# PEER block, dense part: one of the four one-hot products per build step moved from VectorE to ScalarE, key lists searched in another order, activations and gates loaded earlier

## The chip, the cores and the metric

One core of one Trainium2 chip runs the whole program. The time is the device time of one execution in microseconds, the median over several runs; a lower time is better. The engines that matter here are TensorE (PE in the profile), VectorE (DVE), ScalarE (ACT), GpSimd (POOL, which issues the gathers) and SyncE (SP, which issues most loads).

## The reference, cut to what matters

Two transformer blocks run on 512 tokens of 1024 features. The second ends with PEER, a layer of 16384 small experts that are addressed by two lists of 128 keys in each of 8 heads. This is the part that the change touches:

```python
def peer(xn, wq, subkeys, u_tab, v_tab):
    q = (xn @ wq).reshape(bsz, s, PEER_HEADS, 2, PEER_HALF)
    sub = jnp.einsum('bshpd,hpnd->bshpn', q, subkeys, preferred_element_type=jnp.float32)
    s_top, i_top = lax.top_k(sub, PEER_TOPK)
    cand = (s_top[..., 0, :, None] + s_top[..., 1, None, :]).reshape(bsz, s, PEER_HEADS, PEER_TOPK * PEER_TOPK)
    cand_idx = (i_top[..., 0, :, None] * N_KEYS + i_top[..., 1, None, :]).reshape(...)
    best, pos = lax.top_k(cand, PEER_TOPK)
    expert = jnp.take_along_axis(cand_idx, pos, axis=-1)
    gate = jax.nn.softmax(best, axis=-1)
    ...
        a = jax.nn.gelu(jnp.einsum('td,ted->te', xb, u_tab[eb]))
        return jnp.einsum('te,ted->td', (gb * a).astype(vb.dtype), v_tab[eb])
```

There are 16 lists of 128 scores for each block of 128 tokens (8 heads, two halves), so 64 lists in all, and 16 of each are kept.

## The kernel before, in words

The 512 tokens are four blocks of 128, called tb 0 to 3. For the tokens of tb 0, tb 1 and the first half of tb 2 (320 tokens) every expert is computed densely; the other 192 tokens gather their experts' rows from memory.

**Precise matmuls.** `unit()` loads a 128x1024 block of weights on SP's queue, casts the high half on ScalarE (L138, `whi`) and subtracts the low half on VectorE (L140, `wlo`), in rings of four; `mm3` makes each product as three matmuls (L156 to L158). So each block of weights passes ScalarE, then VectorE, then TensorE.

**Query stage.** Sixteen projections give the queries; after each, TensorE makes the key scores `sub`. Between them `advance(route, ...)` hands out pieces of the generator `routed()`, whose first pieces search the lists of tb 2 and 3 (`top_keys`, five VectorE instructions for a list).

**u stage.** A loop over 50 pairs of expert blocks calls `u_block` 100 times: 24 matmuls of 128x320, then a gelu on ScalarE into `ab` (L879). Four such blocks are stored to `a_dram` at a time. Beside each block the loop advances `routed()` by the time `R_US` and the gathers by `GATHER`. `routed()` makes, in this order: `keys` of tb 2 and of tb 3, the 32 lists of tb 0 and 1, `keys` and `build` of tb 0, the same of tb 1, `weights2` (which needs all 64 of the first gathers, L891), and `build` of tb 2.

**Build steps.** A step of `build` serves 8 tokens. VectorE makes two one-hot tiles (`oh1` L1036, `oh2` L1037) and two products of `oh2`, with the high half of the gates (`ohh`) and with the low half (`ohl`), both in L1043. TensorE multiplies them into two banks, 8 tokens by two 128x128 f16 matmuls (L1050); ScalarE moves each bank to `gt` (L1051). There are 40 such plain steps (16 for tb 0, 16 for tb 1, 8 for tb 2); eight "made" steps of tb 2 have three products. Every second step ends with two copies to `gres` (L1055) and a store to `g_dram`.

**v stage.** For each of 128 expert blocks `v_block` runs 18 matmuls of 128x512. `first` fetches stored activations (`al`) from `a_dram` or computes the block there and then; `second` fetches a group of gates (`gl`, one for eight blocks) and multiplies the two on VectorE (L1170), then splits the product (L152, L153). These loads stand in SP's queue among those of the weights. The later gathers (L899, L906) run beside it.

Each engine carries out its instructions in one fixed list, which the framework's scheduler writes when the program is built; the numbers that `yield` hands to `advance` set how many pieces of `routed()` stand beside each block.

Of the kernel before, what the change touches and what calls it, by code (L numbers as in the profile page):

```python
# [9 lines left out]
F32 = mybir.dt.float32  # L10
# [13 lines left out]

TOP_US = 5.0

R_US = 3.6
GATHER = 0.5
G_US = 2.3
NSPILL = 100  # L30
# [30 lines left out]
def tile_layers(ctx: ExitStack, tc: tile.TileContext, A: dict, out: bass.AP):  # L61
# [161 lines left out]
    def zipped(*gs):  # L223
        gs = list(gs)
        while gs:
            for g_ in list(gs):
                t = next(g_, None)
                if t is None:
                    gs.remove(g_)
                else:  # L230
                    yield t
# [621 lines left out]
    drp = pool("peerd", space=DRAM)  # L853
    h_dram = drp.tile([3, 128, 1024], F32, name="h_dram")
    g_dram = drp.tile([16 - N_RES, 128, 24, 8, 16], F32, name="g_dram")
    a_dram = drp.tile([32, 128, 4, N_U], F32, name="a_dram")

    def xs4(tb):
        if tb < 3:
# [61 lines left out]
    def keys(pr, tb):  # L921
# [83 lines left out]
        for j in range(2):  # L1005
            T.transpose(pt[:, 256 + j * 128:384 + j * 128], sl[:, j], ident)
        S.copy(sTs[tb], pt.rearrange("p (a t) -> p a t", a=4))
        if tb == 2:
            S.activation(gT2, pt[:, 320:384], AF.Copy, scale=2.0 ** -14)
        yield 3.0  # L1010
# [13 lines left out]
    def build(pr, tb):  # L1024

        sT = sTs[tb]
        for ts in range(8):
            gt = pr.tile([128, 128, 16], F32, name="gt", bufs=2)
            for t8 in range(0, 16, 8):
                made = tb == 2 and ts >= 4  # L1030
                part = lambda x, t: x[:, t:t + 8].rearrange("p (g q) -> p g q", g=4)[:, :, None, :].to_broadcast([128, 4, 128, 2])
                t0 = ts * 16 + t8
                oh1 = pr.tile([128, 4, 128, 2], F16, name="oh1", bufs=2)
                oh2 = pr.tile([128, 4, 128, 2], F16, name="oh2", bufs=1)
                io = iota16[:, None].to_broadcast([128, 4, 128, 2])
                V.tensor_tensor(oh1, io, part(sT[:, 0], t0), op=OP.is_equal)  # L1036
                V.tensor_tensor(oh2, io, part(sT[:, 1], t0), op=OP.is_equal)  # L1037
                ohs = []
                for name in ("ohh", "ohl", "ohm")[:3 if made else 2]:
                    o_ = pr.tile([128, 4, 128, 2], F16, name=name, bufs=1 if name == "ohm" else 2)  # L1040
                    o_ = o_.bitcast(BF16) if made else o_[:]
                    x_ = part(w2s[:, len(ohs)], t0 - 64) if made else part(sT[:, 2 + len(ohs)], t0)
                    V.tensor_tensor(o_, oh2, x_, op=OP.mult)  # L1043
                    ohs.append(o_)
                for q in range(2):
                    gp = bank("b").rearrange("p (t i) -> p t i", t=4)
                    for j in range(4):
                        g2, t2 = 2 * q + j // 2, j % 2
                        for o_ in ohs:
                            T.matmul(gp[:, j, :], o_[:, g2, :, t2], oh1[:, g2, :, t2], start=o_ is ohs[0], stop=o_ is ohs[-1])  # L1050
                    S.activation(gt[:, :, t8 + 4 * q:t8 + 4 * q + 4], gp.rearrange("p t i -> p i t"), AF.Copy,  # L1051
                                 scale=1.0 if made else 2.0 ** -14)
                yield 3.4 if made else 2.7
            for g in range(N_RES):
                S.copy(gres[g][:, tb * 8 + ts], gt[:, 8 * g:8 * g + 8, :])  # L1055
            nc.scalar.dma_start(g_dram[:, :, tb * 8 + ts].rearrange("g p i t -> p g (i t)"),
                                gt[:, 8 * N_RES:, :].rearrange("p (g i) t -> p g (i t)", i=8))
# [3 lines left out]
    with ExitStack() as st:  # L1061
        ptop = pool("ptop", stack=st)
        sTs = {tb: ptop.tile([128, 4, 128], F16, name=f"sT{tb}") for tb in (0, 2)}
        sTs[1] = sTs[0]
        gT2 = ptop.tile([128, 64], F32, name="gT2")
        w2s = ptop.tile([128, 3, 64], BF16, name="w2s")
        zg = ptop.tile([128, 128], F32, name="zg")
# [16 lines left out]
               pk.tile([128, 16, 128], F32, name=f"sub{tb}") for tb in range(4)]  # L1084
        skT = pk.tile([128, 16, 128], F32, name="skT")
        nc.scalar.dma_start(skT, A["skT"])
        todo = []

        def routed():
            while todo or not keyed:  # L1090
                if todo:
                    yield from todo.pop(0)
                else:
                    yield 0.0
            st2.close()
            pr = pool("pr", stack=st)
            yield from keys(pr, 2)
            yield from keys(pr, 3)
            for tb in (0, 1):
                yield from top_keys(sub[tb], tb, range(16))  # L1100
            for tb in (0, 1):
                yield from keys(pr, tb)
                yield from build(pr, tb)
            while not made2:
                next(gat)
            weights2()
            yield 0.5
            yield from build(pr, 2)
# [4 lines left out]
        for c4 in range(4):  # L1113
            sb_ = [bank("b") for _ in range(4)]
            for j in range(4):
                hp = c4 * 4 + j
                qc = pk.tile([128, 512], F32, name="qc", bufs=2)
                S.copy(qc, pr4[j] if c4 == 0 else proj_T(next_unit(), xhi, xlo))
                for tb in range(4):
                    T.matmul(sb_[tb][:, j * 128:(j + 1) * 128], qc[:, tb * 128:(tb + 1) * 128], skT[:, hp, :],  # L1120
                             start=True, stop=True)
                if c4:
                    d1 = advance(route, d1 + TOP_US)
            for tb in range(4):
                S.copy(sub[tb][:, c4 * 4:c4 * 4 + 4, :], sb_[tb].rearrange("p (a n) -> p a n", a=4))
            todo += [top_keys(sub[tb], tb, range(c4 * 4, c4 * 4 + 4)) for tb in (2, 3)]
        keyed.append(True)
        for n4 in range(0, 2 * len(SPAIR), 4):
            ab = ptop.tile([128, 4, N_U], F32, name="ab", bufs=2)
            for j in range(4):  # L1130
                u_block(2 * SPAIR[(n4 + j) // 2] + j % 2, ab[:, j, :], "a")

                if ready:
                    g1 = GATHER * (2 - len(made2))
                    d2 = advance(gat, d2 + g1)
                d1 = advance(route, d1 + R_US - (g1 if ready else 0.0))
            nc.scalar.dma_start(a_dram[n4 // 4], ab)
        for _ in route:
            pass

    with ExitStack() as st:
        pv = pool("pv", stack=st)
        yb_ = [[bank("a") for _ in range(2)] for _ in range(2)] + [[bank("b") for _ in range(2)]]
        state = {"debt": 0.0}

        def first(p, j):

            if j == 0:
                if p in SPAIR:
                    n = SPAIR.index(p)  # L1150
                    if n % 2 == 0:
                        state["al"] = pv.tile([128, 4, N_U], F32, name="al", bufs=2)
                        nc.sync.dma_start(state["al"], a_dram[n // 2])
                    state[p] = state["al"][:, 2 * (n % 2):2 * (n % 2) + 2, :]
                else:
                    state[p] = pv.tile([128, 2, N_U], F32, name="av", bufs=2)
            if p not in SPAIR:
                u_block(2 * p + j, state[p][:, j, :], "b")

        def second(p):  # L1160

            i1 = 2 * p
            if i1 % 8 == 0 and i1 // 8 < N_RES:
                state["gl"] = gres[i1 // 8]
            elif i1 % 8 == 0:
                state["gl"] = pv.tile([128, 24, 8, 16], F32, name="gl", bufs=2)
                nc.sync.dma_start(state["gl"], g_dram[i1 // 8 - N_RES])
            av = state.pop(p)
            g4 = state["gl"][:, :, i1 % 8:i1 % 8 + 2, :]
            V.tensor_tensor(g4[:, 0:N_U // 16], av.rearrange("p b (s t) -> p s b t", t=16), g4[:, 0:N_U // 16], op=OP.mult)  # L1170
            whi = pv.tile([128, 2, 384], F32R, name="wvhi", bufs=3)
            wlo = pv.tile([128, 2, 384], F32R, name="wvlo", bufs=3)
            split(whi.rearrange("p b (s t) -> p s b t", t=16), wlo.rearrange("p b (s t) -> p s b t", t=16), g4)
            return whi, wlo

        def v_block(i1, w):
            vu = unit(A["peer_v"][i1 * 128:(i1 + 1) * 128, :])
            for tb in range(3):
                for hf in range(2):
                    mm3(yb_[tb][hf], w[0][:, i1 % 2, tb * 128:(tb + 1) * 128], w[1][:, i1 % 2, tb * 128:(tb + 1) * 128],  # L1180
                        vu[0][:, hf * 512:(hf + 1) * 512], vu[1][:, hf * 512:(hf + 1) * 512], i1 == 0, i1 == 127)

        for j in range(2):
            first(0, j)
        w = second(0)
        first(1, 0)
        for p in range(64):
            g_us = G_US if p in SPAIR else 1.5 * G_US
            if p < 63:
                first(p + 1, 1)  # L1190
                wn = second(p + 1)
            v_block(2 * p, w)
            state["debt"] = advance(gat, state["debt"] + g_us)
            if p < 62:
                first(p + 2, 0)
            v_block(2 * p + 1, w)
            state["debt"] = advance(gat, state["debt"] + g_us)
            w = wn
# [138 lines left out]
```

## Time and profile before

| what | us |
|---|---|
| median of 3 runs (lowest, highest) | 2135.93 (2133.8, 2136.33) |
| the profiled execution, own time | 2130.1 |
| its span in the trace | 2128.4 |
| TensorE busy (share) | 2048.3 (96%) |
| VectorE busy (share) | 1575.3 (74%) |
| ScalarE busy (share) | 821.0 (39%) |
| GpSimd busy (share) | 524.3 (25%) |

The span is that of the trace; the execution's own time is 1.7 us longer. Busy time is a sum over instructions, and matmuls overlap, so a stage is better read by its stretches. Stretches that the text names, in us from the start of the span: the query stage 946 to 1047, the u stage 1051 to 1480 (its part with `keys` and lists until 1229, its part with build steps from there), the v stage 1500 to 2121.

### The profile page before, as it was taken

Reading aid. Unit: us, or ns where it says so; the run is one execution under the profiler, and the core shown is the slowest. Engines: PE = TensorE matmul, PEld = TensorE weight load, DVE = VectorE, ACT = ScalarE, POOL = GpSimd, SP = SyncE. Lnnn points to the kernel's source line nnn. Section 1 sums busy time; section 2 is a strip of 40 time slices with the busy share of each in tenths; the row PEclk is TensorE's granted clock in tenths of the full one; section 3 lists DMA queues with packets and bytes.
Section 4 is the critical chain, followed back from the end, with each engine's and each line's share of the span. In section 5 each row is a group of like instructions: output and inputs, shape, how many; then the busy total and the mean of one; then the engine's idle time right before and its main releaser. Section 6 shows DMA issues by size and latency. Waiting matters only on the chain.

```text
span 2128.4 us, 29432 instructions
## 1 busy us (share of the span) xinstructions
PE 2048.3 (96%) x11104; PEld 1743.5 (82%) x11104; DVE 1575.3 (74%) x2880; ACT 821.0 (39%) x1303; POOL 524.3 (25%) x383
## 2 busy tenths in 40 slices
PE   7979999999988999999989999999999999999999
PEld 6737888888876877888889899999888878788887
DVE  6994633332259955455699999998898988899997
ACT  4364422221244342333453455555333333233332
POOL 1000100000010000000032222220575666566573
PEclk9989999999999999999999999999999999999999
DMA  5202233333222222333278899899999999999996
GB/s 190 78 21 89 80 99 98 92 98 118 81 79 80 75 84 70 109 124 99 84 282 280 288 301 359 295 364 303 373 393 410 392 404 392 410 391 410 412 405 241
DMA packets 163282, 476.47 MB, mean 224 GB/s; under 512 B 13866, under 2 KB 57266, under 8 KB 161219
## 3 DMA queue, kind: packets, MB, share of 16 engines
q1 hardware_dynamic: 67104, 259.70, 34.4%
q0 software_dynamic: 46656, 169.18, 20.8%
q10 hardware_dynamic: 49378, 45.71, 6.3%
q8 instruction: 87, 1.43, 0.3%
q14 instruction: 57, 0.46, 0.1%
HBM read 432.18 MB, written 42.09 MB: 223 GB/s over the span
## 4 chain that ended last, share of the span: by engine, by line
PE 25%; DVE 18%; issue 14%; DMA 10%; POOL 3%; ACT 1%; DVEq 0%; POOLq 0%; SPq 0%; ACTq 0%
PE bank_a L158 5%; PE bank_a L156 5%; PE bank_a L157 5%; DVE wlo L140 5%; DMA rows<-in_peer_u_dram,gidx 3%; POOL rows L883 3%; DMA rows<-in_peer_v_dram,gidx 3%; DVE rows L899 2%; DMA al<-a_dram 2%; PE bank_b L156 2%; PE bank_b L157 2%; PE bank_b L158 2%; DVE rows L891 2%; PE bank_b L1050 1%; DMA raw<-in_ut_dram 1%
## 5 line engine op out<-in xcount | busy, mean ns | idle before, releaser
L138 ACT CAST whi<-raw 128x1024 fp32r<-128x1024 f32 (+1 forms) x413 | 431.9, 1047 | 891.4 <-PE bank_a L157 327.3
L140 DVE TENSOR_TENSOR wlo<-raw,whi 128x1024 fp32r<-128x1024 f32 (+1 forms) x413 | 500.1, 1214 | 274.1 <-ACT whi L138 271.8
L156 PE MATMUL bank_a<-xhi,whi 128*128 128x320 f32 (+2 forms) x1600 | 548.2, 344 | 1.0 <-ACT xhi L152 0.8
L158 PE MATMUL bank_a<-xhi,wlo 128*128 128x320 f32 (+2 forms) x1600 | 545.1, 341 | 4.0 <-DVE wlo L140 3.7
L157 PE MATMUL bank_a<-xlo,whi 128*128 128x320 f32 (+2 forms) x1600 | 547.1, 342 | 0.6 <-DVE xlo L153 0.6
L883 POOL DMA_INDIRECT rows<-in_peer_u_dram,gidx x192 | 280.9, 1463 | 554.2 <-DVE gidx L984 145.0
L158 PEld LDWEIGHTS bank_a<-xhi,wlo 128*128 128x128 f32 x1600 | 302.2, 189 | 32.9 <-DVE wlo L140 6.0
L156 PEld LDWEIGHTS bank_a<-xhi,whi 128*128 128x128 f32 x1600 | 301.6, 189 | 29.3 <-issue 2.0
L157 PEld LDWEIGHTS bank_a<-xlo,whi 128*128 128x128 f32 x1600 | 302.7, 189 | 27.1 <-DVE xlo L153 1.6
L883 POOL DMA_INDIRECT rows<-in_peer_v_dram,gidx x128 | 207.0, 1617 | 115.2 <-DVE h L906 90.3
L164 POOL TENSOR_TENSOR rstd<-rstd,neghalf 128x1 f32<-128x1 f32 (+2 forms) x37 | 26.6, 720 | 826.2 <-DVE rstd L163 818.2
L156 PE MATMUL bank_a<-whi,wvhi 128*128 128x512 f32 x512 | 201.1, 393 | 8.2 <-ACT wvhi L152 8.1
L158 PE MATMUL bank_a<-whi,wvlo 128*128 128x512 f32 x512 | 201.4, 393 | 1.9 <-DVE wvlo L153 1.9
L157 PE MATMUL bank_a<-wlo,wvhi 128*128 128x512 f32 x512 | 200.6, 392 | 2.4 <-DVE wlo L140 2.4
L906 DVE SCALAR_TENSOR_TENSOR h<-rows,ga,h 128x1024 f32<-128x1024 f32 x128 | 164.3, 1284 | 5.2 <-DMA rows<-in_peer_v_dram,gidx 4.2
L899 DVE SCALAR_TENSOR_TENSOR rows<-rows,h 128x1024 f32<-128x1024 f32 x128 | 152.8, 1220 | 7.7 <-DMA rows<-in_peer_u_dram,gidx 7.7
L156 PEld LDWEIGHTS bank_a<-whi,wvhi 128*128 128x128 f32 x512 | 96.9, 189 | 29.1 <-ACT wvhi L152 10.2
L158 PEld LDWEIGHTS bank_a<-whi,wvlo 128*128 128x128 f32 x512 | 96.7, 189 | 25.1 <-DVE wvlo L153 5.1
L157 PEld LDWEIGHTS bank_a<-wlo,wvhi 128*128 128x128 f32 x512 | 96.8, 189 | 22.4 <-DVE wlo L140 3.2
L157 PE MATMUL bank_b<-wlo,wvhi 128*128 128x512 f32 x256 | 99.6, 389 | 0.0
L156 PE MATMUL bank_b<-whi,wvhi 128*128 128x512 f32 x256 | 99.6, 389 | 0.0
L158 PE MATMUL bank_b<-whi,wvlo 128*128 128x512 f32 x256 | 99.6, 389 | 0.0
(400 smaller groups left out, 3255.2 us busy)
## 6 DMA issues: line engine op xcount, KB each, us to landing
raw<-in_wt_dram SPq DMA_DIRECT2D x150, 512.0 KB
raw<-in_ut_dram SPq DMA_DIRECT2D x128, 512.0 KB
raw<-in_peer_v_dram SPq DMA_DIRECT2D x128, 512.0 KB
g_dram<-gt ACTq DMA_DIRECT2D x24, 896.0 KB
gl<-g_dram SPq DMA_DIRECT2D x14, 1536.0 KB
a_dram<-ab ACTq DMA_DIRECT2D x25, 640.0 KB
al<-a_dram SPq DMA_DIRECT2D x25, 640.0 KB
rows<-in_peer_u_dram,gidx POOLq DMA_INDIRECT x192
```

The lines of the kernel that those rows point to most:

```text
L138: lead[0] = S.copy(hi[:, :n], raw[:, :n]).ins
L140: pace[0] = V.tensor_tensor(lo[:, :n], raw[:, :n], hi[:, :n].bitcast(F32), op=OP.subtract).ins
L156: T.matmul(o, lh, rh, start=start, stop=False)
L157: T.matmul(o, lh, rl, start=False, stop=False)
L158: T.matmul(o, ll, rh, start=False, stop=stop)
L164: G.tensor_tensor(r, r, neghalf[:, :shape[1]], op=OP.pow)
L883: G.indirect_dma_start(out=r, out_offset=None, in_=table, in_offset=bass.IndirectOffsetOnAxis(ap=idx[:, k:k + 1], axis=0))
L891: V.scalar_tensor_tensor(r, r, 1.0, hn2, op0=OP.mult, op1=OP.mult, accum_out=ga2[:, k:k + 1])
L899: V.scalar_tensor_tensor(r, r, 1.0, hn3, op0=OP.mult, op1=OP.mult, accum_out=ga[:, k:k + 1])
L906: V.scalar_tensor_tensor(h[3], r, ga[:, k:k + 1], h[3], op0=OP.mult, op1=OP.add)
L1050: T.matmul(gp[:, j, :], o_[:, g2, :, t2], oh1[:, g2, :, t2], start=o_ is ohs[0], stop=o_ is ohs[-1])
```

## The change

It does four things. (1) In the 40 plain build steps the product with the low half of the gates, one VectorE instruction of 128x1024, becomes eight ScalarE instructions of 128x128, each scaled by one column of `glo`, a new f32 copy of the low halves; `oh2` gets a second buffer. (2) The lists are kept in two queues, in pieces of two; those of tb 0 and 1 can now be searched in the query stage when those of tb 2 and 3 have been, and what is left of them alternates with `keys` of tb 2 and 3. (3) `R_US` becomes 3.3, and a plain step's `yield` 2.1. (4) Activations are stored and loaded in pairs, loaded four pairs ahead into five buffers; a group of gates is loaded three pairs earlier.

```diff
-R_US = 3.6
+R_US = 3.3
@@
         S.copy(sTs[tb], pt.rearrange("p (a t) -> p a t", a=4))
+        S.copy(glo[tb], pt[:, 384:512])
@@
-                oh2 = pr.tile([128, 4, 128, 2], F16, name="oh2", bufs=1)
+                oh2 = pr.tile([128, 4, 128, 2], F16, name="oh2", bufs=2)
@@
-                    V.tensor_tensor(o_, oh2, x_, op=OP.mult)
+                    if made or name == "ohh":
+                        V.tensor_tensor(o_, oh2, x_, op=OP.mult)
+                    else:
+                        for t in range(8):
+                            S.mul(o_[:, t // 2, :, t % 2], oh2[:, t // 2, :, t % 2], glo[tb][:, t0 + t:t0 + t + 1])
@@
-                yield 3.4 if made else 2.7
+                yield 3.4 if made else 2.1
@@
-            yield from keys(pr, 2)
-            yield from keys(pr, 3)
-            for tb in (0, 1):
-                yield from top_keys(sub[tb], tb, range(16))
+            yield from zipped(chain(keys(pr, 2), keys(pr, 3)), chain(*todo[1]))
@@
-            todo += [top_keys(sub[tb], tb, range(c4 * 4, c4 * 4 + 4)) for tb in (2, 3)]
+            for tb in (2, 3, 0, 1):
+                todo[tb < 2] += [top_keys(sub[tb], tb, range(c4 * 4 + j, c4 * 4 + j + 2)) for j in (0, 2)]
@@
-        for n4 in range(0, 2 * len(SPAIR), 4):
-            ab = ptop.tile([128, 4, N_U], F32, name="ab", bufs=2)
+        for n, p in enumerate(SPAIR):
+            ab = ptop.tile([128, 2, N_U], F32, name="ab", bufs=2)
@@
-            nc.scalar.dma_start(a_dram[n4 // 4], ab)
+            nc.scalar.dma_start(a_dram[n], ab)
@@
+        def load_a(p):
+
+            if p in SPAIR:
+                state[p] = pv.tile([128, 2, N_U], F32, name="al", bufs=5)
+                nc.sync.dma_start(state[p], a_dram[SPAIR.index(p)])
+
+        def load_g(g):
+
+            if g < N_RES:
+                state["g", g] = gres[g]
+            elif g < 16:
+                state["g", g] = pv.tile([128, 24, 8, 16], F32, name="gl", bufs=2)
+                nc.sync.dma_start(state["g", g], g_dram[g - N_RES])
@@
-            if i1 % 8 == 0 and i1 // 8 < N_RES:
-                state["gl"] = gres[i1 // 8]
-            elif i1 % 8 == 0:
-                state["gl"] = pv.tile([128, 24, 8, 16], F32, name="gl", bufs=2)
-                nc.sync.dma_start(state["gl"], g_dram[i1 // 8 - N_RES])
+            if i1 % 8 == 0:
+                state["gl"] = state.pop(("g", i1 // 8))
+            if i1 % 8 == 2:
+                load_g(i1 // 8 + 1)
@@
+            if 5 <= p + 4 < 64:
+                load_a(p + 4)
             v_block(2 * p, w)
```

The first place is ScalarE's list in the build steps of tb 0. Before, it holds these rows (`ab` is the gelu after a block of 24 matmuls, `whi` the cast that a later block needs, `gt` the copies that a build step's matmuls end with):

```order
L879 ACTIVATE ab<-bank_a 128x320
L138 CAST whi<-raw 128x1024 x2
L879 ACTIVATE ab<-bank_a 128x320
L1051 ACTIVATE gt<-bank_b 128x128x4 x2
L1137 DMA a_dram<-ab 128x1280
L138 CAST whi<-raw 128x1024
L879 ACTIVATE ab<-bank_a 128x320
L1051 ACTIVATE gt<-bank_b 128x128x4 x2
L1055 COPY gres_6485<-gt 128x128
L1055 COPY gres_6486<-gt 128x128
L1056 DMA g_dram<-gt 128x14x128
```

The casts stand two to four blocks ahead of the gelus there: the tile that is cast between two gelus is not that of the next block. After the change, the pattern that repeats for two blocks and two steps is this one:

```order
L879 ACTIVATE ab<-bank_a 128x320
L1048 ACTIVATE ohl<-oh_10365,glo_7070 128x128 x3
L1056 ACTIVATE gt<-bank_b 128x128x4 x2
L1143 DMA a_dram<-ab 128x640
L138 CAST whi<-raw 128x1024
L1048 ACTIVATE ohl<-oh_10437,glo_7070 128x128 x8
L1056 ACTIVATE gt<-bank_b 128x128x4
L138 CAST whi<-raw 128x1024
```

There are 16 scaling instructions (L1048) in it, and the number of casts ahead has shrunk: from the fifth block of a build on, the first of these two casts is that of the very next block, and it stands behind the gelu of the block before and behind both copies of the step between them.

The second place is VectorE's list ahead of `weights2`, where the last of the first gathers (L891) are taken in. Before:

```order
L1043 TENSOR_TENSOR ohl<-oh_12326,sT_7068 128x1024
L891 SCALAR_TENSOR_TENSOR rows,ga_6475<-rows,h_71 128x1024
L140 TENSOR_TENSOR wlo<-raw,whi 128x1024
L891 SCALAR_TENSOR_TENSOR rows,ga_6475<-rows,h_71 128x1024 x4
L899 SCALAR_TENSOR_TENSOR rows,ga<-rows,h_70 128x1024
```

And after:

```order
L1038 TENSOR_TENSOR oh_12463<-iota_7088,sT_7069 128x1024
L140 TENSOR_TENSOR wlo<-raw,whi 128x1024
L891 SCALAR_TENSOR_TENSOR rows,ga_6475<-rows,h_71 128x1024 x15
L140 TENSOR_TENSOR wlo<-raw,whi 128x1024
L891 SCALAR_TENSOR_TENSOR rows,ga_6475<-rows,h_71 128x1024 x2
L1037 TENSOR_TENSOR oh_12462<-iota_7088,sT_7069 128x1024
```

Fifteen gather products now stand between two low halves of weights, where four and one stood.

Counted over the same lists: of the 32 lists of tb 0 and 1 none stood in the query stage before, and 14 do now. `build` of tb 0 began after 44 gelus of the u stage and begins after 37 now; before, build steps stood beside the blocks up to the end of the stage, and now the last seven blocks have none beside them.

The third place is SP's queue at the start of the v stage, as a difference:

```order
-L1153 DMA al<-a_dram 128x1280
+L1156 DMA al<-a_dram 128x640 x2
 L134 DMA raw<-in_peer_v_dram 128x1024
-L1153 DMA al<-a_dram 128x1280
-L1167 DMA gl<-g_dram 128x3072
+L1156 DMA al<-a_dram 128x640 x2
+L1164 DMA gl<-g_dram 128x3072
 L134 DMA raw<-in_ut_dram 128x1024
 L134 DMA raw<-in_peer_v_dram 128x1024
-L1167 DMA gl<-g_dram 128x3072
+L1156 DMA al<-a_dram 128x640 x2
+L1164 DMA gl<-g_dram 128x3072
```

The same bytes are loaded, in pieces of half the size, and a piece stands further ahead of the block that uses it.

## Rows read from the trace of the kernel before

**Rows 1.** Stretches by stage: start, length, busy us of each engine (instructions), clock, DMA

```profile
946.00:1047.00 101.00, 100.76 (x567) 85.80 (x566) 49.09 (x212) 33.04 (x49) 0.00 (x0) 1.00 0.29 92
1051.00:1229.00 178.00, 166.77 (x1171) 161.21 (x1171) 174.38 (x675) 81.30 (x113) 44.61 (x36) 0.99 0.76 269
1229.00:1480.00 251.00, 247.30 (x2154) 241.29 (x2153) 247.34 (x435) 142.42 (x261) 50.92 (x41) 0.99 0.95 326
1500.00:2121.00 621.00, 608.01 (x2854) 512.78 (x2853) 563.26 (x639) 209.72 (x236) 386.77 (x240) 0.99 0.99 390
```

**Rows 2.** Waits of TensorE, 1051 to 1480: us in total, times, longest

```profile
PE bank_b L976 <- DVE ohl L973: 9.3, 5, 2.5
PE bank_a L158 <- DVE wlo L140: 3.7, 7, 0.9
```

**Rows 3.** Waits of TensorE and of VectorE, 1500 to 2121

```profile
PE bank_a L156 <- ACT wvhi L152: 8.1, 3, 3.6
...
DVE gl L1170 <- DMA al<-a_dram: 20.1, 5, 4.8
...
DVE gl L1170 <- DMA gl<-g_dram: 5.6, 3, 3.1
```

**Rows 4.** Timeline of ScalarE in the build part: start, us, instruction

```profile
1261.06 1.05 ACT L138 CAST whi<-raw 128x1024 fp32r<-128x1024 f32 x1 [1.86 <-PE bank_a L157]
1262.01 0.43 ACT L879 ACTIVATE ab<-bank_a 128x320 f32<-128x320 f32 x1
1262.34 0.59 ACT L1051 ACTIVATE gt<-bank_b 128x512 f32<-128x512 f32 x1
...
1262.82 0.60 ACT L1051 ACTIVATE gt<-bank_b 128x512 f32<-128x512 f32 x1
1263.45 0.30 ACT L1055 COPY gres<-gt 128x128 f32<-128x128 f32 x1
...
1263.65 0.29 ACT L1055 COPY gres<-gt 128x128 f32<-128x128 f32 x1
```

**Rows 5.** ScalarE's scaling by a column elsewhere in the program: timeline, and group

```profile
19.61 0.98 ACT L344 ACTIVATE dg<-cst,cw 128x128 f32<-128x128 f32 x3
...
L344 ACT ACTIVATE dg<-cst,cw 128x128 f32<-128x128 f32 x8 | 3.0, 397 | 1.5 <-PE bank_b L345 1.4
```

**Rows 6.** Timeline of TensorE in the build part (ten f16 matmuls between the first two rows)

```profile
1232.55 0.22 PE L1050 MATMUL bank_b<-oh,ohh 128*128 128x128 f16 x1
...
1233.18 0.22 PE L1050 MATMUL bank_b<-oh,ohh 128*128 128x128 f16 x1
...
1233.49 0.30 PE L157 MATMUL bank_a<-xlo,whi 128*128 128x320 f32 x1
1233.64 0.31 PE L158 MATMUL bank_a<-xhi,wlo 128*128 128x320 f32 x1
```

**Rows 7.** Timeline of VectorE ahead of `weights2`

```profile
1404.51 1.22 DVE L140 TENSOR_TENSOR wlo<-raw,whi 128x1024 fp32r<-128x1024 f32 x1
1405.64 1.22 DVE L891 SCALAR_TENSOR_TENSOR rows<-rows,h 128x1024 f32<-128x1024 f32 x1
...
1406.79 1.22 DVE L891 SCALAR_TENSOR_TENSOR rows<-rows,h 128x1024 f32<-128x1024 f32 x1
...
1411.37 0.68 DVE L1036 TENSOR_TENSOR oh<-iota,sT 128x1024 f16<-128x1024 f16 x1
1411.98 0.68 DVE L1037 TENSOR_TENSOR oh<-iota,sT 128x1024 f16<-128x1024 f16 x1
```

**Rows 8.** Groups of VectorE by shape, 1051 to 1480: busy us, mean ns

```profile
L915 DVE FIND_INDEX8 si<-sv,gres 128x8 uint32<-128x128 f32 x32 | 9.2, 287 | 0.0
L914 DVE MAX8 sv<-gres 128x8 f32<-128x128 f32 x32 | 8.9, 282 | 0.0
```

**Rows 9.** TensorE after a wait: timeline (in brackets the idle time before), and the stretch behind it

```profile
1325.93 0.61 PE L976 MATMUL bank_b<-ident,ohl 128*128 128x128 f16 x4 [2.50 <-DVE ohl L973]
...
1326.00:1329.40 3.40, 3.40 (x22) 3.25 (x23) 2.65 (x6) 1.91 (x2) 0.00 (x0) 0.51 0.69 278
```

More of the change, by code (lines that the diff above doesn't have):

```diff
@@ L855, in tile_layers @@
     g_dram = drp.tile([16 - N_RES, 128, 24, 8, 16], F32, name="g_dram")
-    a_dram = drp.tile([32, 128, 4, N_U], F32, name="a_dram")
+    a_dram = drp.tile([64, 128, 2, N_U], F32, name="a_dram")
     def xs4(tb):
@@ L1064, in tile_layers @@
         sTs[1] = sTs[0]
+        glo = {tb: ptop.tile([128, 128], F32, name=f"glo{tb}") for tb in (0, 2)}
+        glo[1] = glo[0]
         gT2 = ptop.tile([128, 64], F32, name="gT2")
@@ L1086, in tile_layers @@
         nc.scalar.dma_start(skT, A["skT"])
-        todo = []
+        todo = [[], []]
         def routed():
-            while todo or not keyed:
-                if todo:
-                    yield from todo.pop(0)
+            while todo[0] or not keyed:
+                if todo[0] or todo[1]:
+                    yield from (todo[0] or todo[1]).pop(0)
                 else:
@@ L1125, in tile_layers @@
                 S.copy(sub[tb][:, c4 * 4:c4 * 4 + 4, :], sb_[tb].rearrange("p (a n) -> p a n", a=4))
-            todo += [top_keys(sub[tb], tb, range(c4 * 4, c4 * 4 + 4)) for tb in (2, 3)]
+            for tb in (2, 3, 0, 1):
+                todo[tb < 2] += [top_keys(sub[tb], tb, range(c4 * 4 + j, c4 * 4 + j + 2)) for j in (0, 2)]
         keyed.append(True)
-        for n4 in range(0, 2 * len(SPAIR), 4):
-            ab = ptop.tile([128, 4, N_U], F32, name="ab", bufs=2)
-            for j in range(4):
-                u_block(2 * SPAIR[(n4 + j) // 2] + j % 2, ab[:, j, :], "a")
+        for n, p in enumerate(SPAIR):
+            ab = ptop.tile([128, 2, N_U], F32, name="ab", bufs=2)
+            for j in range(2):
+                u_block(2 * p + j, ab[:, j, :], "a")
                 if ready:
@@ L1144, in tile_layers @@
         state = {"debt": 0.0}
-        def first(p, j):
[L1148 to L1156, printed above, removed]
+        def load_a(p):
[8 more added lines that the diff above has]
+                nc.sync.dma_start(state["g", g], g_dram[g - N_RES])
+        def first(p, j):
+            if j == 0 and p not in SPAIR:
+                state[p] = pv.tile([128, 2, N_U], F32, name="av", bufs=2)
             if p not in SPAIR:
@@ L1181, in v_block @@
                         vu[0][:, hf * 512:(hf + 1) * 512], vu[1][:, hf * 512:(hf + 1) * 512], i1 == 0, i1 == 127)
+        load_g(0)
+        for p in range(5):
+            load_a(p)
         for j in range(2):
```

## The prediction

> **What bounds the kernel now.** I read the stretches by stage first. In the query stage TensorE is busy for 100.8 of 101 us and VectorE for only 49 [rows 1]: TensorE sets the time and VectorE has half the stage free. In the part of the u stage with keys and lists VectorE is busy for 174.4 of 178 us and TensorE for 166.8, so VectorE sets the time there; the waits say the same, 9.3 us of TensorE behind the one-hot products of `keys` and 3.7 us behind low halves of weights [rows 2]. In the build part both are full, TensorE 247.3 and VectorE 247.3 of 251, while ScalarE is busy for 142.4 [rows 1]. TensorE's own work there is close to that: a matmul of 128x320 starts 0.147 us after the one before (1233.49, 1233.64 and on), so a block of 24 takes 3.53 us; eleven f16 matmuls from 1232.55 to 1233.18 make 0.057 each, so a plain step of 16 takes 0.92 and a made one of 24 takes 1.38 [rows 6]. In the v stage TensorE is busy for 608 of 621 us [rows 1], and what it waits for most is the high half of the gated activations, 8.1 us in three waits; VectorE waits 20.1 us for `al` and 5.6 us for `gl` ahead of the product from which that half is made [rows 3].
>
> So there is little to win: 178 − 167 and 251 − 247 in the u stage, some 15 us, and 13 us in the v stage.
>
> **Lists in the query stage.** A list is five instructions of about 0.28 us each (8.9 and 9.2 us for 32) [rows 8], 1.4 us busy, 1.2 with their overlap. Fourteen of them go into the query stage: 17 to 20 us beside 49 busy of 101, hidden by TensorE's projections. I cost that at 0; if they delayed low halves there, at most the 20 us that they take.
>
> **Keys and lists in the u stage.** This part is now beside 37 blocks instead of 44. VectorE loses the 14 lists (17) and seven blocks' low halves and gathers, 7 x (1.13 + 1.15) = 16 [rows 7]: 174.4 − 33 = 141. TensorE needs 37 x 3.53 = 131 plus the matmuls of `keys` (166.8 − 44 x 3.53 = 11.5): 142. I take 142 us.
>
> **ScalarE in the build steps.** One VectorE product costs 0.61 us (1411.37 to 1411.98) [rows 7]; 40 of them are 24 us, taken from an engine that is full. In their place stand 320 scalings of 128x128 by a column. Three of that kind elsewhere take 0.98 us with 0.397 for one, so they start (0.98 − 0.40)/2 = 0.29 apart [rows 5]. The lower bound is a copy of the same size without the column, 0.20 apart (1263.45, 1263.65) [rows 4]; the upper one is the whole 0.40. I take 0.29, the row of the same operation. For two blocks and two steps ScalarE then has two casts (0.95 apart), two gelus (0.33), four `gt` copies (0.48), two `gres` copies (0.20) [rows 4] and 16 scalings: 2 x 1.28 + 1.92 + 0.40 + 4.64 = 9.5 us (8.1 at 0.20, 11.3 at 0.40). TensorE needs 2 x (3.53 + 0.92) = 8.9. The sum alone is nearly a tie.
>
> The Trainium skill, "ScalarE: Activation LUTs", Rules for kernel authors, says to put a plain product on VectorE, and budgets about 0.3 us for an instruction with a pointer operand plus 0.83 ns per element. By it one scaling would be an estimated 0.41 us, which is the 0.397 that the row gives for one by itself but not the 0.29 between starts; the sum for two blocks would be 11.4 us instead of 9.5.
>
> What costs more than the sum is the order. ScalarE's list shows the cast of the next block behind the gelu of the block before, which needs the end of that block on TensorE, and behind both `gt` copies. So the chain closes on itself once for two blocks: the last matmul's tail 0.16 (0.31 long, next start 0.15 later) [rows 6], gelu 0.33, three scalings 0.87, two `gt` 0.96, cast 1.05 [rows 4], low half 1.22 [rows 7], then the block's other 22 matmuls 3.23 with half a step 0.46 between, and the next block 3.53: **11.8 us** in place of 8.9, 2.9 lost each time. At a scaling of 0.20 it is 11.5, and without the wait for the low half (two matmuls run ahead of it) not under 10.8, a loss of 2. Before, the casts stood two to four blocks ahead, so the chain was open.
>
> **The u stage summed.** Keys 142. Each of the two long builds spans 16 blocks; the first four have their casts ahead (17.8 at 8.9 a pair), and the other twelve are six closed pairs, 71: 89 each, 178. `keys` of tb 1 between them, 8 blocks, 30. Then `weights2`: 17 gather products in two runs stand ahead of the low halves, 17 x 1.15 = 19.5 [rows 7], of which a block in hand covers 3.5, so 16 lost; the plain steps of tb 2 beside six blocks, 27 at TensorE's pace plus about one closed pair 3: 46. Eight made steps with ten blocks, 10 x 3.53 + 8 x 1.38 = 46. Seven blocks with nothing beside them, 25. Together 467 us against 178 + 251 = 429: **+38**. The last seven blocks are where VectorE's saved time ends up: the routing is finished early, and nothing is there to shorten.
>
> The second `oh2` costs no time by itself: VectorE's one-hots would otherwise wait for ScalarE's readers. The copy into `glo` (three, at most 0.6 each) lies in VectorE's time. A smaller `R_US` with a smaller yield only sets the order that is counted above.
>
> **The v stage.** Activations four pairs ahead and gates three take away VectorE's 20.1 + 5.6 [rows 3]; what reaches the end is bounded by TensorE's idle time, 621 − 608 = 13, and starts at 0 since DMA is busy for 0.99 of the stage [rows 1]: a load that is issued earlier then takes its share from the weights. I take **−9**, the 8.1 behind the high half and some of the rest [rows 3]. Loads of half the size are not slower by anything that a row shows.
>
> **The sum.** 38 − 9 = +29. The profiled execution had 2130.1 of its own, so 2159; the median of the runs shown is 5.8 higher, so **2165**.
>
> **Rivals.**
> (a) *The casts keep their lead on the chip.* If fewer pairs are closed than I count, the change gains. Without any, the u stage is 467 − 13 x 2.9 = 429, no change, and with −9 the time is 2127, faster. It turns at about three closed pairs (3 x 2.9 = 9). For it: VectorE loses 24 + 17 us of work in a stage that it fills. Against: a list is carried out in order, and 13 such pairs stand in it. The Trainium skill, "Perfetto Trace Analysis", Optimizing Scalar/DVE Operations, says that moving work to ScalarE may make sense where VectorE is saturated. By that rule it would be this case; the trace agrees on the 98%, and it shows TensorE equally full.
> (b) *The closed pairs cost less, since gather products and pieces of `keys` are drawn into the gaps.* At 2 us for 13 pairs (−12), 8 for the run of gathers (−8), and all 13 us of the v stage (−4) the time is 2141, just slower; with ScalarE at 0.20 as well, within the bound of no change, 2136.
> (c) *TensorE's clock drops in the gaps.* After a wait of 2.50 us it ran at 0.51 of its full clock for 3.4 us, losing 1.7 [rows 9]. The gap in a closed pair is about 2.1 (second `gt` 0.48, cast 1.05, and the way to them), followed by two matmuls and a wait for the scalings. If it drops in each, 14 x 1.7 = 24: 2189.
> (d) *The earlier loads bring nothing*, because the queues are as full as before: +9, 2174.
>
> **How the numbers follow.** A chance of 0.52 for the forecast (its own range 2152 to 2178), 0.11 for (a), 0.11 for (b), 0.15 for (c), 0.11 for (d). The range from 2137 to 2189 leaves out (a) and the upper end of (c). Time differences under 0.2% (4 us) can't be told from no change by a measurement of this kernel. Faster: (a) and a small part of (b), 0.13. Same: half of (b), 0.06. Slower: 0.81.
>
> **What will show it.** In the u stage after: the scalings 0.29 us apart; the waits of TensorE led by high halves from ScalarE's cast (L138), 2 us at a time in the builds, some 12 of them, where before there were none; pairs of gelus 11.8 apart instead of 9; one idle stretch of TensorE of some 16 us ahead of `weights2`; the first to the last gelu 467 us. The keys part would be 142 long and the last seven blocks 3.5 each. In the v stage the waits for `al` and `gl` are gone and TensorE is idle for 4 us instead of 13. The prediction is wrong if the gelus in the builds keep a distance of 4.5 us (then (a)), or if the granted clock shows halves all along the builds (then (c)).

## The result and the profile after

The changed kernel takes 2223.28 us (median of 4 runs, 2219.39 to 2224.01) against 2134.86 for the kernel before in the same series: ratio 1.0415, 95% interval 1.04 to 1.0429. It is slower, as forecast, but by 88 us where 29 were summed; the time lies above the range.

The stretches of the changed kernel by stage: start and end, length, busy us of PE, PEld, DVE, ACT, POOL (instructions), clock, DMA share, GB/s. They answer to [rows 1].

```profile
946.00:1047.00 101.00, 100.76 (x567) 85.83 (x567) 66.26 (x324) 32.77 (x48) 0.00 (x0) 1.00 0.29 93
1051.00:1193.00 142.00, 131.86 (x958) 130.31 (x958) 140.14 (x573) 70.18 (x98) 28.47 (x24) 0.98 0.74 257
1193.00:1585.00 392.00, 335.56 (x2416) 302.55 (x2416) 254.70 (x397) 249.20 (x605) 72.78 (x57) 0.89 0.76 249
1605.00:2215.00 610.00, 603.28 (x2827) 509.91 (x2827) 552.82 (x623) 208.84 (x234) 370.88 (x233) 0.99 0.98 388
```

The query stage took 17 us more of VectorE's work at no cost. All of the loss is in the build part: TensorE busy for 336 of 392 us, where it was busy for 247 of 251, and its granted clock 0.89. The first and the last gelu of the u stage, before and then in the changed kernel:

```profile
L879 ACT ACTIVATE ab<-bank_a x100: 421/433/479, 1050.9 to 1479.6; 128x320 f32<-128x320 f32 x100
```

```profile
L879 ACT ACTIVATE ab<-bank_a x100: 410/436/443, 1051.2 to 1584.6; 128x320 f32<-128x320 f32 x100
```

So the u stage, from the first to the last of them, is 533.4 us long instead of 428.7: +104.7. What lies behind it is 637.6 instead of 648.8: −11.2. TensorE's waits in the u stage of the changed kernel (total, times, longest):

```profile
PE bank_b L1055 <- DVE ohh L1045: 24.6, 15, 1.7
PE bank_a L158 <- DVE wlo L140: 9.5, 4, 8.9
PE bank_b L1055 <- ACT ohl L1048: 8.8, 17, 1.7
PE bank_a L156 <- ACT whi L138: 8.6, 4, 2.7
...
PE bank_b L1006 <- DVE slot L1001: 6.3, 1, 6.3
```

The first row names a VectorE product, fifteen times up to 1.7 us. It is the release that came last by a little; the cast that came just ahead of it is seen in the timeline of one pair of blocks, here of all engines in the changed kernel:

```profile
1262.97 0.44 ACT L879 ACTIVATE ab<-bank_a 128x320 f32<-128x320 f32 x1 [1.66 <-PE bank_a L158]
...
1266.96 0.44 ACT L879 ACTIVATE ab<-bank_a 128x320 f32<-128x320 f32 x1 [2.10 <-PE bank_a L158]
...
1267.29 1.01 ACT L1048 ACTIVATE ohl<-oh,glo 128x128 f16<-128x128 f16 x3
...
1268.34 0.69 DVE L1038 TENSOR_TENSOR oh<-iota,sT 128x1024 f16<-128x1024 f16 x1 [3.66 <-ACT ohl L1048]
...
1268.64 0.59 ACT L1056 ACTIVATE gt<-bank_b 128x512 f32<-128x512 f32 x1
...
1269.12 1.05 ACT L138 CAST whi<-raw 128x1024 fp32r<-128x1024 f32 x1
...
1269.55 0.69 DVE L1045 TENSOR_TENSOR ohh<-oh,sT 128x1024 f16<-128x1024 f16 x1
...
1270.20 1.23 DVE L140 TENSOR_TENSOR wlo<-raw,whi 128x1024 fp32r<-128x1024 f32 x1
1270.29 0.29 PE L1055 MATMUL bank_b<-oh,ohh 128*128 128x128 f16 x2 [1.70 <-DVE ohh L1045]
1270.39 0.39 PE L156 MATMUL bank_a<-xhi,whi 128*128 128x320 f32 x1
...
1271.48 0.62 PE L158 MATMUL bank_a<-xhi,wlo 128*128 128x320 f32 x1
...
1271.90 0.47 PE L156 MATMUL bank_a<-xhi,whi 128*128 128x320 f32 x1
1272.17 0.47 PE L157 MATMUL bank_a<-xlo,whi 128*128 128x320 f32 x1
```

The closed pair is there, step for step: gelu, three scalings, the copies, the cast (until 1270.17), and TensorE's next matmul 0.1 us behind it. A second strand comes in at the same time: VectorE's one-hot `oh2` (L1038) waits 3.66 us until ScalarE's scalings have read the tile's older buffers, and `ohh`, the product that the next build matmul needs, is done at 1270.24, 0.07 us behind the cast. TensorE is idle for 1.70 us, and from 1271.48 its matmuls start 0.27 apart instead of the 0.147 of [rows 6]. The stretches of two such pairs, by the same columns as above:

```profile
1249.40:1263.00 13.60, 11.69 (x84) 10.40 (x82) 7.44 (x10) 9.82 (x27) 0.94 (x1) 0.87 0.71 224
1263.00:1276.60 13.60, 11.69 (x84) 10.40 (x81) 8.59 (x12) 9.79 (x27) 2.19 (x2) 0.87 0.82 237
```

A pair takes 13.6 us at a mean clock of 0.87. It holds one stretch of 3.4 us at half the clock, which costs 1.7 us at most; without it the pair is 11.9, and 11.8 was worked out. ScalarE is busy for 9.8 us in it. The scalings start 0.29 apart, as taken.

Ahead of `weights2` stand these idle times of TensorE (timeline):

```profile
1454.57 0.42 PE L156 MATMUL bank_a<-xhi,whi 128*128 128x320 f32 x1 [2.62 <-ACT whi L138]
...
1469.50 0.64 PE L158 MATMUL bank_a<-xhi,wlo 128*128 128x320 f32 x1 [8.86 <-DVE wlo L140]
```

The stretch around them:

```profile
1453.00:1478.00 25.00, 11.58 (x59) 9.65 (x60) 21.67 (x39) 8.94 (x20) 20.13 (x17) 0.59 1.00 377
```

Of 25 us TensorE works in 11.6, at a mean clock of 0.59.

### The profile page after: what moved, and what is told of

Its sections match the earlier page's. It is cut to its first block, busy times and chain, and to the rows that moved or that the text cites. A ratio compares the mean times of both kernels' runs of the same rounds, so it can differ in the third digit from the quotient of the medians.

```text
span 2222.2 us, 29782 instructions
## 1 busy us (share of the span) xinstructions
PE 2097.1 (94%) x11104; PEld 1771.2 (80%) x11104; DVE 1559.0 (70%) x2840; ACT 913.1 (41%) x1626; POOL 518.5 (23%) x383
## 4 chain that ended last, share of the span: by engine, by line
PE 34%; issue 16%; DVE 13%; DMA 4%; POOL 4%; ACT 1%; DVEq 0%; POOLq 0%; ACTq 0%; SPq 0%
PE bank_a L158 8%; PE bank_a L156 8%; PE bank_a L157 7%; POOL rows L883 4%; DVE wlo L140 3%; PE bank_b L156 3%; PE bank_b L157 3%; PE bank_b L158 3%; DVE rows L899 2%; DMA raw<-in_peer_v_dram 2%; DMA rows<-in_peer_u_dram,gidx 1%; PE bank_b L1055 1%; DVE h L906 1%; DMA raw<-in_ut_dram 1%; DVE wvlo L153 1%
## 5 line engine op out<-in xcount | busy, mean ns | idle before, releaser
L156 PE MATMUL bank_a<-xhi,whi 128*128 128x320 f32 (+2 forms) x1600 | 561.0, 352 | 9.5 <-ACT whi L138 8.6
L158 PE MATMUL bank_a<-xhi,wlo 128*128 128x320 f32 (+2 forms) x1600 | 556.6, 348 | 9.8 <-DVE wlo L140 9.5
L157 PE MATMUL bank_a<-xlo,whi 128*128 128x320 f32 (+2 forms) x1600 | 557.7, 349 | 0.6 <-DVE xlo L153 0.6
L156 PEld LDWEIGHTS bank_a<-xhi,whi 128*128 128x128 f32 x1600 | 311.5, 195 | 38.5 <-ACT whi L138 10.3
L158 PEld LDWEIGHTS bank_a<-xhi,wlo 128*128 128x128 f32 x1600 | 311.4, 195 | 37.7 <-DVE wlo L140 11.5
L157 PEld LDWEIGHTS bank_a<-xlo,whi 128*128 128x128 f32 x1600 | 312.2, 195 | 27.0 <-DVE xlo L153 1.7
L883 POOL DMA_INDIRECT rows<-in_peer_v_dram,gidx x128 | 196.9, 1538 | 119.9 <-DVE h L906 101.8
L1048 ACT ACTIVATE ohl<-oh,glo 128x128 f16<-128x128 f16 x320 | 104.6, 433 | 5.6 <-DVE oh L1038 5.5
```

The lines of the kernel that those rows point to most:

```text
L156: T.matmul(o, lh, rh, start=start, stop=False)
L157: T.matmul(o, lh, rl, start=False, stop=False)
L158: T.matmul(o, ll, rh, start=False, stop=stop)
L883: G.indirect_dma_start(out=r, out_offset=None, in_=table, in_offset=bass.IndirectOffsetOnAxis(ap=idx[:, k:k + 1], axis=0))
L1048: S.mul(o_[:, t // 2, :, t % 2], oh2[:, t // 2, :, t % 2], glo[tb][:, t0 + t:t0 + t + 1])
```

## The experiments

**The low product back on VectorE.** The changed kernel with

```diff
-                    if made or name == "ohh":
-                        V.tensor_tensor(o_, oh2, x_, op=OP.mult)
-                    else:
-                        for t in range(8):
-                            S.mul(...)
+                    V.tensor_tensor(o_, oh2, x_, op=OP.mult)
```

> The changed kernel with the low product back as one VectorE instruction (all else of the change kept, the run of 15 gather products too). Theory (the scalings let ScalarE's casts fall back to a lead of none, which closes the chain cast, block, gelu, cast, and the gaps halve TensorE's clock): pairs of gelus back at 9 us, about two half-clock periods in the u stage, u stage 425 to 440 instead of 533, median about 2125. Rival (the run of gathers ahead of weights2 and the uneven filling of the blocks cost most of it): u stage over 470, median over 2160.

2139.48 us, ratio 1.0026 (1.0015 to 1.0038). The u stage is 445.9 us, with pairs of 9.0 and one interval of 31.7 ahead of `weights2`:

```profile
L879 ACT ACTIVATE ab<-bank_a x100: 420/432/450, 1051.9 to 1497.8; 128x320 f32<-128x320 f32 x100
```

So the scalings cost 533 − 446 = 87 us, nearly the whole loss. The median is 14 above what was expected: the run of gathers keeps its price when the scalings are gone.

**The scalings without the lists.** The kernel before with the loads, the f32 copy `glo` and

```diff
-                oh2 = pr.tile([128, 4, 128, 2], F16, name="oh2", bufs=1)
+                oh2 = pr.tile([128, 4, 128, 2], F16, name="oh2", bufs=2)
@@
-                    V.tensor_tensor(o_, oh2, x_, op=OP.mult)
+                    if made or name == "ohh":
+                        V.tensor_tensor(o_, oh2, x_, op=OP.mult)
+                    else:
+                        for t in range(8):
+                            S.mul(...)
```

> The kernel before with the scalings on ScalarE and the loads of the v stage changed (which make room for the second one-hot tile), but with the lists, R_US and the yields of before; only four gather products in a row ahead of weights2. Theory: the list shows the casts without a lead here as well, so the u stage is 490 to 520 and the median about 2190 to 2210. Rival (the gather run and the filling cost most): u stage under 460, median under 2150.

2222.87 us, ratio 1.0422 (1.0404 to 1.0439), u stage 522.3: the loss comes with the scalings alone, and is 13 us above the range expected, which no run explains. No run of 15 gather products is in it. The loads by themselves take 2134.2 us (below).

**Casts two blocks ahead.** The changed kernel with

```diff
+        blocks = [2 * p + j for p in SPAIR for j in range(2)]
+        early = [unit(A["ut"][i]) for i in blocks[:2]]
@@
-                u_block(2 * p + j, ab[:, j, :], "a")
+                if 2 * n + j + 2 < len(blocks):
+                    early.append(unit(A["ut"][blocks[2 * n + j + 2]]))
+                u_block(2 * p + j, ab[:, j, :], "a", early.pop(0), lead[0])
```

where `u_block` puts its gelu behind the cast it is given.

> The changed kernel, but the weights of a block are asked for two blocks early and a gelu is placed behind the cast of the block two later, so the lead is two throughout. Theory: no closed pairs, pairs at ScalarE's sum of 9.5 to 10, few half-clock periods, u stage 440 to 465, median 2130 to 2155. Rival (320 small instructions are too much work for ScalarE whatever their order): pairs over 11, u stage over 490, median over 2180.

2216.01 us, ratio 1.039 (1.0363 to 1.0418): the expectation fails, and with it the theory as it stood. By the ratios some 5 us are won, within the two intervals. The casts are ahead, yet a pair takes 13.9 us. ScalarE's timeline in this kernel:

```profile
1260.35 2.47 ACT L1049 ACTIVATE ohl<-oh,glo 128x128 f16<-128x128 f16 x8
...
1264.91 0.60 ACT L1057 ACTIVATE gt<-bank_b 128x512 f32<-128x512 f32 x1 [1.65 <-PE bank_b L1056]
1265.40 1.04 ACT L138 CAST whi<-raw 128x1024 fp32r<-128x1024 f32 x1
...
1267.05 2.50 ACT L1049 ACTIVATE ohl<-oh,glo 128x128 f16<-128x128 f16 x8
1271.77 1.22 ACT L1057 ACTIVATE gt<-bank_b 128x512 f32<-128x512 f32 x2 [2.22 <-PE bank_b L1056]
```

And the stretch of about a pair:

```profile
1260.00:1274.10 14.10, 12.46 (x83) 9.97 (x84) 7.71 (x11) 10.21 (x28) 0.94 (x1) 0.88 0.69 213
```

Now the copies (`gt`) wait for TensorE, and the next step's eight scalings stand behind them. That is a second loop: scalings, build matmuls, copies, next scalings. From the copy at 1264.91 to the end of the scalings at 1269.55 ScalarE works for 4.6 us without a gap, while TensorE has one block of 3.5. The profile ends TensorE's wait by VectorE here too (timeline of the same kernel):

```profile
1272.39 0.69 DVE L1038 TENSOR_TENSOR oh<-iota,sT 128x1024 f16<-128x1024 f16 x1 [2.12 <-PE bank_b L1056]
...
1273.74 0.29 PE L1056 MATMUL bank_b<-oh,ohh 128*128 128x128 f16 x2 [1.39 <-DVE ohh L1046]
```

The one-hot waits for the build matmuls before it, and `ohh` follows at once. So the cast's lead took only 0.3 us from the gap of 1.70: `ohh` ends it now as it did before. Which strand of the second loop sets the pair, the copies with the next scalings or the one-hots with `ohh`, no run separates; a third buffer of the one-hot tiles was not tried.

**Scalings ahead, casts as they fall.** The changed kernel with the copies of a step put behind the scalings of the step after it:

```diff
-                            S.mul(o_[...], oh2[...], glo[tb][...])
+                            last = S.mul(o_[...], oh2[...], glo[tb][...]).ins
+                while late:
+                    late.pop(0)(None if made else last)
@@
-                    S.activation(gt[...], gp.rearrange("p t i -> p i t"), AF.Copy, ...)
+                    late.append(copy)
```

where `copy` is that activation, ordered behind `last`, and the `gres` copies and the store follow it in the same list.

> The changed kernel with the copies of a step's banks behind the scalings of the next step, but the casts left as they fall, without a lead in the builds. Theory (either loop closes by itself, so opening one of them is not enough): pairs 12 to 13.6 with a half-clock period each, median 2195 to 2222. Rival (only the loop through the scalings mattered): pairs under 10.5, median about 2173.

2224.1 us, ratio 1.0416 (1.0395 to 1.0437), pairs of 14.2 to 15.6 us, both above the ranges expected: opening this loop alone wins nothing.

**Both.** Casts two blocks ahead and copies behind the next scalings.

> As the kernel with the casts two blocks ahead, and in addition the copies of a build step's banks are put behind the scalings of the step after it, so that ScalarE scales a step ahead of TensorE. Theory (it was a loop through both engines, and with the casts ahead the loop scalings, build matmuls, copies, next scalings closed instead): both loops are open now, a pair costs ScalarE's own 9.5 to 10.3, no half-clock periods in the builds, u stage 455 to 475, median 2145 to 2165. Rival (ScalarE can't do 320 more instructions in this stage in any order): pairs over 11.5, u stage over 500, median over 2190.

2173.15 us, ratio 1.0188 (1.0174 to 1.0203): 50 us back, only 8 above the range expected. The u stage is 478.5 us. ScalarE's timeline in this kernel, from the gelu of a block to that of the block two later:

```profile
1234.63 0.43 ACT L880 ACTIVATE ab<-bank_a 128x320 f32<-128x320 f32 x1
1234.96 2.48 ACT L1050 ACTIVATE ohl<-oh,glo 128x128 f16<-128x128 f16 x8
1237.31 1.06 ACT L1062 ACTIVATE gt<-bank_b 128x512 f32<-128x512 f32 x2
1238.26 1.05 ACT L138 CAST whi<-raw 128x1024 fp32r<-128x1024 f32 x1
...
1244.34 0.43 ACT L880 ACTIVATE ab<-bank_a 128x320 f32<-128x320 f32 x1
```

And the stretch of this pair:

```profile
1234.63:1244.34 9.71, 9.71 (x77) 8.49 (x77) 7.19 (x11) 9.68 (x27) 2.07 (x2) 1.00 1.02 330
```

ScalarE works back to back, 9.68 of 9.71 us, the clock is full, and a pair takes 9.7 us (9.5 was its sum). With both loops open ScalarE is the bound, 0.7 above TensorE's 9.0.

**The gap filled.** The changed kernel with ten idle matmuls ahead of the waiting block:

```diff
+        for _ in range(fill):
+            with order(built[0]):
+                T.matmul(o, xhi8[:, 0, 0:128], xhi8[:, 0, 0:N_U], start=True, stop=True)
```

in 24 of the blocks; they add work that no result uses.

> The changed kernel with ten idle matmuls of 128x320 (1.47 us, their result is overwritten) in TensorE's list in the gap of each closed pair, behind the last build step and ahead of the block that waits for its cast. Theory with the clock (a gap of 1.7 us in a pair is enough to halve it for 3.4 us, 1.7 lost each): the pairs of 13.6 become 11.9 to 12.2 without half-clock periods, median 2190 to 2205 in spite of 240 more matmuls. Rival (the pair's length is the chain's alone, the clock loses nothing that the chain waits for): pairs 13.6 or longer, median 2223 or more.

2220.12 us, ratio 1.0402 (1.0385 to 1.0419). The median misses its range, the pair does not: here are gelus two blocks apart in ScalarE's timeline of this kernel:

```profile
1250.62 0.44 ACT L884 ACTIVATE ab<-bank_a 128x320 f32<-128x320 f32 x1 [0.15 <-PE bank_a L158]
...
1262.68 0.44 ACT L884 ACTIVATE ab<-bank_a 128x320 f32<-128x320 f32 x1 [0.17 <-PE bank_a L158]
```

And the stretch of two pairs:

```profile
1240.00:1264.20 24.20, 23.41 (x183) 20.60 (x182) 15.97 (x23) 19.67 (x54) 3.54 (x3) 1.00 0.88 263
```

12.06 us at the full clock instead of 13.6 at 0.87: the idle 1.7 us did cost 1.5 more each time. In all the half-clock time of the u stage fell from 92 to 44 us. The u stage fell by 8 us only (525.3), since about half of the 24 fills stand where there was no gap, and each is 1.47 us there: 24 won, some 17 paid, by estimate.

**The loads, the lists and the gathers.** Five kernels without scalings. The loads alone are part (4) of the diff, the lists alone part (2), on the kernel before; then both; then each of the last two with

```diff
-GATHER = 0.5
+GATHER = 0.62
```

> The kernel before with the loads of the v stage alone changed (activations in pairs four ahead, gates three pairs earlier). Theory: VectorE's waits for al and gl go, and the v stage is shorter by the 8 to 11 us that the changed kernel shows there; u stage as before, 429; median about 2124. Rival (the shorter v stage came from something else, such as the order of the gathers): no change, median 2133.

> The kernel before with the lists alone changed (loads as before, R_US, yields and GATHER too); the run of 15 gather products stands in its list. Theory (the loads bring nothing, and the v stage is shorter where more of the second gathers were taken in during the u stage): as lists and loads together, u stage about 448, stretch behind it 642 to 643 with 10 or 11 of the second gathers taken in earlier instead of 6, median 2141 to 2145. Rival (the loads shorten the v stage): stretch behind the u stage 648, median 2147 to 2151.

> The kernel before with the lists and the loads changed, without scalings on ScalarE and with R_US and yields of before. The run of 15 gather products ahead of weights2 stands in its list. Theory (lists bring VectorE time, and the run takes it back): u stage 425 to 445 with one interval of about 30 us ahead of weights2, median 2122 to 2140. Rival (the lists in the query stage are a plain gain): u stage under 420, median under 2118.

> The kernel before with the lists changed and GATHER 0.62, loads as before. Theory (the loads bring nothing): as with the loads, median 2120 to 2126, u stage 430, stretch behind it 642. Rival (the loads do their part once the u stage is in order): 2128 to 2133.

> As the kernel with lists and loads, and GATHER 0.62 instead of 0.5, so that the first gathers are spread over the fewer blocks and no run stands ahead of weights2. Theory: the interval of 30 us goes, u stage 412 to 422, median 2108 to 2118, the fastest so far. Rival (VectorE is full in any case and the time reappears beside the other blocks): as without it, 2122 to 2140.

| kernel | median us | ratio to before (95%) | u stage | behind it |
|---|---|---|---|---|
| before, in the two series (stages of the profiled execution of 2130.1) | 2132.81, 2134.99 | 1 | 428.7 | 648.8 |
| loads | 2134.2 | 1.0014 (1.0 to 1.0028) | 432.2 | 647.9 |
| lists | 2152.78 | 1.0088 (1.0072 to 1.0103) | 451.2 | 648.3 |
| lists, loads | 2143.26 | 1.0043 (1.0031 to 1.0055) | 447.8 | 641.8 |
| lists, GATHER 0.62 | 2136.78 | 1.0007 (0.9997 to 1.0018) | 433.5 | 650.9 |
| lists, loads, GATHER 0.62 | 2123.07 | 0.9949 (0.9937 to 0.9961) | 430.0 | 642.4 |

The stages are read from one profiled execution of each kernel. No median lies in the range of its theory: the loads alone and the last kernel came out as their rivals had it, the two kernels with lists and without loads lie above both ranges, and lists with loads 3 us above its own. The lists alone lose 18 us through the run of gathers, 27 to 29 us in one interval; with the gathers spread the u stage is 18 us shorter again and the interval gone. But it comes back to 430 to 433, not to 412 to 422: the VectorE time that the lists free is not turned into time, since TensorE is busy for 416 of the 430 us. The loads are worth nothing alone, and by the ratios 10 to 12 us with the lists; lists, loads and spread gathers together are the fastest version here, 2123 us. Part (3) costs little: with the lists, the loads and the new `R_US` and `yield`, the kernel with the low product back takes 2139.48 us, and with the old ones 2143.26. VectorE's waits for the casts in the v stage before, and its waits there with the loads alone:

```profile
DVE wlo L140 <- ACT whi L138: 7.6, 7, 3.8
```

```profile
DVE wlo L140 <- ACT whi L138: 20.9, 13, 4.4
...
DVE gl L1177 <- DMA al<-a_dram: 2.4, 2, 1.6
```

Against [rows 3] 17.7 of the 20.1 us for `al` are gone, and 13.3 more are waited for the casts. That is the outcome of rival (d); its reason, full queues, is not shown. Why the same loads shorten the stage by 6 to 9 us when the lists are changed is not shown: the theory that more gathers taken in beforehand did it fell, since lists without loads take in as many (10 or 11 instead of 6) and their stage is as long as before.

**Both loops open, gathers spread.** GATHER 0.66 on the kernel with both.

> The kernel with both loops open (casts and scalings ahead) and GATHER 0.66, so that no run of gather products stands ahead of weights2. Theory: pairs of 9.7 as without, the interval of 29.5 goes and some 20 to 25 us with it, median 2146 to 2155; still slower than lists and spread gathers without scalings (2123), since a pair is set by ScalarE at 9.7 instead of by TensorE at 9.0. Rival (the run is made good elsewhere, VectorE being full): median over 2160.

2164.81 us, ratio 1.0144 (1.0125 to 1.0162). The u stage falls by 16 us to 462.1, but what lies behind it rises from 639.2 to 650.7; the expected median is missed for that, the time lies where the rival had it, and the stage behind is again not explained. The scalings remain a loss in either form.

## Why the prediction was wrong

The direction was right, and a part of the mechanism: ScalarE's list closes a loop through TensorE, pairs of blocks stretch, the last seven blocks have nothing to shorten. By the terms of the sum:

- Query stage, 0: held. Scaling at 0.29: held. Made steps 46 (measured 46.1 for the same ten blocks) and last blocks at 3.52: held. v stage −9: measured −11.2, but the size says nothing for the reason, since the loads alone move the waits and win no time; that it came near is luck as far as these runs show.
- Keys part, 142: measured 150.9. TensorE waited 6.3 us in one place for a gate (L1006 behind L1001, shown above) that was worked out in alternation with lists; before, this wait was 0.3 us. With the lists and the old `R_US` it is 1.4, so the alternation alone does not make it.
- **The two builds, 178: the step that failed.** A pair was put at 11.8 with the clock at full speed; it takes 13.6. I had set the drop of the clock aside as rival (c) with a chance of 0.15, because the gap was computed at 2.1 us and the row I had was a drop after 2.50 [rows 9]. In the runs a gap of 1.70, and in the kernel with the casts ahead one of 1.39, was enough in most of the pairs. The first build took 108.8 us instead of 89, the second 105.1 up to its last block: 36 above the 178. TensorE ran at half speed for 51 us of the two, which costs 26 at most. Besides, two intervals of 10.6 to 13.1 us in each build, where eight or eleven scalings and two or four copies stand between a gelu and the next cast, were not counted.
- The run ahead of `weights2`, 16 lost: the interval is 26.4 us (25 to 32 in the other kernels with the run), some 22 lost, 20 us of it at half the clock.
- Two terms besides: `keys` of tb 1, 30, took 36.0; `weights2` with the plain steps of tb 2, 46, took 61, the run included. With the keys part (9) and the builds (36) these make the 66 us that the u stage exceeds its forecast. In all it ran at half the clock for 92 us, in 16 stretches, against 7 before. So rival (c), 24 us for the pairs alone, would have been too small as well.
- The second `oh2` was put at nothing, with the reason that VectorE's one-hots would otherwise wait for ScalarE. They wait in spite of it: 27.6 us in nine waits between 1201 and 1300.
- Rival (b), the gaps being filled by other work, did not happen; (a) did not, the list was kept.

One more error is not in the sum but in the reason: I took the missing lead of the casts for the cause. Restored alone it wins next to nothing, since `ohh` comes as late as the cast did, and the copies and scalings seem to close a loop of their own; only with both orders changed does a pair fall to 9.7. Shown is that the scalings cost 87 us of the u stage, that both orders have to change, that this gives back 50, that the drop of the clock costs 1.5 us in a pair, and that the run of gathers costs some 20. Left open is which strand sets the second loop, and how the loads and the lists act together in the v stage.

## What to carry to other kernels

Before work is moved to an engine that looks half idle, write down its list for one period and follow who waits for whom: an engine at 57% that stands between two stages of a loop can add its whole time to the loop, and opening one loop can leave another closed. When pieces of work are moved forward, see what was paced by the blocks that they leave; here gathers piled up ahead of their reader, and a number (GATHER) mended it. A recurring gap of TensorE has to be priced at its clock, too.

## What the runs showed of the hardware

Neither the length of a wait nor its recurrence tells by itself whether TensorE's clock falls. In the kernel before, one wait of 2.0 us, which ended at 1220.7, left the clock at full speed; TensorE's wait from 1218 on (total, times, longest) and the stretch behind it:

```profile
PE bank_b L976 <- DVE ohl L973: 2.0, 1, 2.0
```

```profile
1220.70:1224.10 3.40, 3.40 (x33) 3.33 (x34) 3.40 (x8) 3.37 (x5) 0.14 (x1) 1.00 0.93 371
```

The same wait in the kernel with the loads alone, as long and ended at 1224.9, was followed by half the clock:

```profile
PE bank_b L976 <- DVE ohl L973: 2.0, 1, 2.0
```

```profile
1225.40:1228.80 3.40, 3.40 (x20) 3.26 (x18) 2.95 (x8) 3.00 (x4) 0.00 (x0) 0.50 0.97 388
```

In the changed kernel most of the gaps of 1.70 us that came back every 13.6 us brought 3.4 us at half the clock (1.2 of 2.4 GHz), and matmuls without any use put into the gap kept it full. In the kernel with only the scalings ahead the clock fell in the pairs although no single gap in the pair below is longer than 0.72 us:

```profile
1231.98 0.23 PE L1058 MATMUL bank_b<-oh,ohl 128*128 128x128 f16 x1 [0.72 <-ACT ohl L1049]
...
1235.59 0.64 PE L156 MATMUL bank_a<-xhi,whi 128*128 128x320 f32 x1 [0.72 <-ACT whi L138]
```

```profile
1231.00:1245.40 14.40, 12.42 (x83) 10.24 (x82) 8.50 (x12) 9.91 (x26) 2.40 (x2) 0.88 0.73 218
```

The Trainium skill, "TensorE: Matmul & The Clock Gate", A second HAM failure mode: psum-queue depth-cycling, tells of a kernel in which short idle times between groups of matmuls, often enough, move the clock back and forth; the traces agree, with 0.87 over a pair and 1.00 with the gap filled.
